# A two-layer sequence trunk on one core: the planner that orders its instructions gets measured durations instead of guessed ones

## The chip, the core and the metric

One core of a Trainium2 chip runs the whole program once. The metric is the device time of one execution in microseconds (us), the median over several. The engines are TensorE (PE), VectorE (DVE), ScalarE (ACT), GpSimd (POOL) and SyncE (SP); each works through its own instructions strictly in their order, and semaphores tie the engines together.

## What is computed

The input is 2048 tokens of 1024 channels in float32, the output the same. There are two layers with a residual each, and a last RMSNorm:

```
def _even_mixer(h, w_in, ...):                    # layer 0, h = rmsnorm(x)
    proj = jnp.einsum('bsd,de->bse', h, w_in)     # 1024 -> 2048
    u_pool, u_ssm, z = proj[..., :512], proj[..., 512:1024], proj[..., 1024:]
    y_pool = _multiscale_pool(u_pool, pool_w, pool_scale)   # windows 2, 4, 8, 16; 128 channels each
    y_ssm = _s5(u_ssm, ...)     # 32 groups of 16 channels, 64 complex states each, then a GLU
    y = jnp.concatenate([y_pool, y_ssm], axis=-1) * jax.nn.silu(z)
    return jnp.einsum('bse,ed->bsd', y, w_out)    # 1024 -> 1024

def _odd_mixer(h, w_in, ...):                     # layer 1
    val, gt, z = three times 1024 channels of h @ w_in
    g = val * jax.nn.sigmoid(gt)
    c = causal depthwise convolution of g, width 31, + conv_b
    c = layernorm(c) * ln_g + ln_b
    return (silu(c) * silu(z)) @ w_out
```

## The kernel before

**Tiling.** The sequence is worked in two halves, A and B, of 1024 tokens, each in two blocks of 512. A large product is cut into units of 128 output channels for one half. Each weight tile of 128x1024 is loaded (`raw`), cast to a rounded part on ACT and subtracted from the original on DVE, so that a high and a low part (`w`) exist; the activations are split alike. A unit then has 8 (contraction) x 3 (high x high, high x low, low x high) x 2 (blocks) = 48 matmuls of 128x128 by 128x512. Its sum lies in a PSUM slot `mm`, of which there are three, until DVE or ACT has evacuated it.

**PE's units** come in a written order, on the thread `main`: A.s0 to A.s3 (input of the SSM), A.pu0, A.pz0, A.pu1 ... A.pz3 (input of the pooling and its gate), A.z0 to A.z3 (gate of the SSM), the same for B; then A.glu, A.o (output projection of layer 0), A.g, A.v, A.y (layer 1), the same for B, and A.q, B.q (last projection; A.q.e0t0 is its first unit). The first three units of a projection are done block by block (A.s2.0, A.s2.1), as are A.z1 to A.z3. Some hundred smaller pieces of matmuls stand between and inside the units: the tables of the SSM (threads prepw and prepg), the SSM itself (ssm00 and 01 for half A, ssm10 to 12 for half B), the pooling (pool0, pool1), part of the convolution, and the sums of the LayerNorm (lnA0, lnA1, lnB0, lnB1: one for each block).

**What makes the order.** The kernel isn't written in the order in which it runs. Each thread is a generator that yields an operation (`Op`, with its engine, an assumed duration, what it reads and writes), a request for a slot (`Alloc`) or a condition (`Wait`). `Sched.run` plays the program: every engine has a clock (`clk`), `ready` gives the time at which an operation's operands are there, and `run` always takes the operation that can start first; among those of the same engine that can start within a small tolerance (`EPS`) it takes first the ones that aren't of `main`, then those of the higher rank. `emit` advances the clock and writes the instruction. So the durations decide nothing of what is computed, but in which order each engine gets its instructions, which slot each tile lies in, and where a piece stands among the units. On the chip the order is fixed, whatever the real durations are.

**Queues.** All DMAs, loads and stores, are issued by SP in the planned order (`dma`, L342). The slots that tie the engines beside `mm`: 2 `raw`, 8 `w` (four tiles of weights), 8 `st` (scratch), 2 `po` (evacuated sums), 25 `act`, 2 `aux` (PSUM of the small pieces).

**Places the text speaks of.** The SSM's tables are made on DVE from `ca`, `cg` and `pw` in scratch slots (`act16_...<-cg1_...`), sent through small matmuls and stored to DRAM (`Kd`, `Wd`, `Md`); the rates (`act17`, `rsc`) come first. `ud`, `upd`, `z0d` and `zp` are DRAM copies of evacuated units. A pooling step loads `upd`, sums on DVE, splits, loads `z0d`, and only then takes an `mm` slot, has six matmuls done in it, and evacuates it with a product by z0d (L308):

```
        yield dma(sz, z0d[h][gi])
        ps = yield Alloc("mm")
        yield mmb([... six matmuls into ps ...])
...
        yield stt(sz, ps, vc("pool_scale", gi), sz, ALU.mult, ALU.mult)
        free("mm", ps)
```

`rsd` holds the reciprocal norms of 1024 tokens; they are stored as single elements (`sml`, one float for each run) and loaded again, spread over all partitions.

In the profile L290 is DVE's two-operand operation, L308 the three-operand one, L318 the scan, L322 ACT's copy, L333 ACT's activation, L351 the matmul, L342 the DMA. In the changed kernel the same lines are L312, L330, L340, L344, L356, L390 and L375.

Of the kernel before, what the change touches and what calls it, by code (L numbers as in the profile page):

```python
# [73 lines left out]
class Sched:  # L74
# [132 lines left out]

    def run(self):
        while self.threads:
# [13 lines left out]
            est = lambda t: max(self.clk[t.op.eng], t.op.ready)  # L223
            first = min(cand, key=est)
            e0 = est(first)
            eng = first.op.eng
            near = [t for t in cand if t.op.eng == eng and est(t) <= e0 + self.EPS[eng]]
            th = min(near, key=lambda t: (t.bulk, t.prio, est(t)))
# [6 lines left out]
def trunk(ctx, tc, io):  # L235
# [49 lines left out]

    def tt(o, a, b, op, eng=None):
        if eng is G:
            return Op("G", 0.25 + width(o) * 2.1e-3, [a, b], [o], lambda: G.tensor_tensor(o, a, b, op))  # L288
        d = 0.13 + width(o) / 960.0 + (0.13 if isps(a, b) else 0.0)
        return Op("V", d, [a, b], [o], lambda: V.tensor_tensor(o, a, b, op))  # L290

    def ts(o, a, s1, s2=None, op0=ALU.mult, op1=None, eng=None):
# [8 lines left out]
        if eng is G:  # L301
            return Op("G", 0.25 + width(o) * 1e-3, rd, [o], emit)
        return Op("V", 0.15 + width(o) / (960.0 if isps(a) else 1920.0), rd, [o], emit)

    def stt(o, a, s, b, op0, op1):
        rd = [a, b] + ([s] if isinstance(s, bass.AP) else [])
        d = 0.13 + width(o) / 960.0 + (0.13 if isps(a, b) else 0.0)
        return Op("V", d, rd, [o], lambda: V.scalar_tensor_tensor(o, a, s, b, op0, op1))  # L308

    def vcopy(o, a):  # L310
        return Op("V", 0.13 + width(o) / 960.0, [a], [o], lambda: V.tensor_copy(o, a))

    def recip(o, a):
        return Op("V", 0.13 + width(o) / 120.0, [a], [o], lambda: V.reciprocal(o, a))

    def scan(o, r, x, ini):
# [1 line left out]
        return Op("V", 0.13 + width(o) / 480.0, rd, [o], lambda: V.tensor_tensor_scan(  # L318
            o, r.to_broadcast([128, width(o)]), x, ini, ALU.mult, ALU.add))

    def acopy(o, a):
        return Op("A", 0.05 + width(o) / 960.0, [a], [o], lambda: A.copy(o, a))  # L322

    def amul(o, a, m):
        return Op("A", 0.1 + width(o) / 960.0, [a], [o], lambda: A.mul(o, a, m))

    def act(o, a, fn, **kw):
# [9 lines left out]

    def dma(o, i):
        n = int(np.prod(o.shape)) * 4
        run = 4 * min(a.ap[-1][1] if a.ap[-1][0] == 1 else 1 for a in (o, i))  # L340
# [1 line left out]
        return Op("SP", slow * n / 360e3, [i], [o], lambda: SP.dma_start(out=o, in_=i))  # L342
# [19 lines left out]
    def trb(batch):  # L362
# [1443 lines left out]
```

## Time and profile before

| | us |
|---|---|
| median of three runs | 1537.63 (1532.89 to 1539.34) |
| the profiled execution, its own time | 1537.14 |
| its span, first instruction to last | 1535.3 |
| PE busy in the span | 1481.3 |
| DVE busy | 1128.9 |
| ACT busy | 524.2 |
| POOL busy | 103.6 |
| mean granted clock of PE | 0.991 |

A line of an engine's timeline gives the start and the length in us, the instruction with out<-in, and in brackets the idle time before it and whose result ended it. A line of waits reads: engine, tile and source line that waited, `<-` what it waited for: us in total, how often, the longest. A group reads: instructions of one kind, `|` busy us, mean ns of one `|` idle us before them. A bound engine that is busy for most of the span can only gain what it waits and what its clock loses.

### The profile page before, as it was taken

To read this page: it belongs to the slowest core of one execution; us is meant where nothing else is said; L and a number is where in the kernel's file an instruction comes from. 1 tells how busy PE (TensorE), PEld (TensorE's weight loads), DVE (VectorE), ACT (ScalarE), POOL (GpSimd) and SP (SyncE) were. 2 spreads that over 40 slices of the span, in tenths; PEclk is the share of its full clock that TensorE was granted. 3 is DMA by queue.
4 is the path that set the end of the run, shared out by engine and by line. 5 is a ranking of instruction groups with operands and counts; after the bars stand their busy time and mean duration, and the time that the engine had idled before them with its cause. 6 is when DMAs were issued, how large, how long until landed. Compare 5 with 4: busy or idle time off the path is not lost. (4 is left out here: it accounts for less than half of the span.)

```text
span 1535.3 us, 18361 instructions
## 1 busy us (share of the span) xinstructions
PE 1481.3 (96%) x6942; PEld 1213.6 (79%) x6942; DVE 1128.9 (74%) x1318; ACT 524.2 (34%) x829; POOL 103.6 (7%) x313
## 2 busy tenths in 40 slices
PE   5899979999999999999999999999999999999997
PEld 3678768788888888888888888888888888887785
DVE  7882648887877533399999999245997898967652
ACT  6113433122135225311111530352364465443431
POOL 1000010110000002000000000120000000003322
PEclk9999989999999999999999999999999999999999
DMA  8238966877775763223253442623476485956743
GB/s 302 96 97 235 331 193 216 266 239 263 239 252 191 207 229 124 83 83 110 82 111 122 179 164 97 220 83 111 98 177 204 133 284 172 363 206 222 257 158 116
DMA packets 165464, 280.77 MB, mean 183 GB/s; under 512 B 55712, under 2 KB 86144, under 8 KB 165376
## 3 DMA queue, kind: packets, MB, share of 16 engines
q1 hardware_dynamic: 165376, 279.61, 56.1%
q8 instruction: 54, 0.88, 0.2%
q14 instruction: 34, 0.28, 0.1%
HBM read 183.93 MB, written 91.43 MB: 179 GB/s over the span
## 5 line engine op out<-in xcount | busy, mean ns | idle before, releaser
L351 PE MATMUL mm<-act,w 128*128 128x512 f32 x4224 | 1002.3, 397 | 29.0 <-ACT w L322 11.1
L351 PEld LDWEIGHTS mm<-act,w 128*128 128x128 f32 x4224 | 793.1, 189 | 211.8 <-ACT w L322 11.1
L308 DVE SCALAR_TENSOR_TENSOR ca<-cg,cwt,ca 128x1024 f32<-128x1024 f32 (+1 forms) x360 | 397.8, 1106 | 14.5 <-ACT ca L333 4.2
L351 PE MATMUL mm<-w,act 128*128 128x512 f32 x1344 | 318.9, 397 | 1.4 <-DVE w L290 1.4
L351 PEld LDWEIGHTS mm<-w,act 128*128 128x128 f32 x1344 | 253.3, 189 | 60.8 <-DVE w L290 1.9
L322 ACT CAST w<-raw 128x1024 fp32r<-128x1024 f32 (+1 forms) x117 | 121.3, 1038 | 265.8 <-PE mm L351 207.2
L290 DVE TENSOR_TENSOR w<-raw,w 128x1024 fp32r<-128x1024 f32 (+1 forms) x117 | 141.6, 1212 | 51.4 <-ACT w L322 50.1
L333 ACT ACTIVATE junk<-st 128x1024 bf16<-128x1024 f32 (+1 forms) x64 | 54.0, 844 | 135.1 <-DVE st L290 122.3
L290 DVE TENSOR_TENSOR po<-mm,st 128x1024 f32<-128x1024 f32 x32 | 46.6, 1455 | 70.6 <-PE mm L351 65.6
L290 DVE TENSOR_TENSOR st<-st,mm 128x512 f32<-128x512 f32 x48 | 30.9, 684 | 76.0 <-PE mm L351 76.0
L322 ACT COPY st<-aux 128x512 f32<-128x512 f32 (+2 forms) x56 | 25.7, 471 | 129.5 <-PE aux L351 100.8
L322 ACT CAST act<-st 128x512 fp32r<-128x512 f32 (+1 forms) x64 | 51.8, 853 | 46.7 <-DVE st L308 16.6
L333 ACT ACTIVATE act<-act,mask 128x128 f32<-128x128 f32 x192 | 57.8, 390 | 18.8 <-DMA act<-band 18.8
L290 DVE TENSOR_TENSOR act<-st,act 128x512 fp32r<-128x512 f32 (+1 forms) x64 | 56.3, 920 | 3.5 <-ACT act L322 3.3
L308 DVE SCALAR_TENSOR_TENSOR st<-st,mm 128x1024 f32<-128x1024 f32 x24 | 34.4, 1432 | 25.8 <-PE mm L351 25.8
L333 ACT ACTIVATE st<-mm 128x1024 f32<-128x1024 f32 x24 | 24.6, 1026 | 83.2 <-PE mm L351 81.0
L308 DVE SCALAR_TENSOR_TENSOR act<-aux,vcol,act 128x512 fp32r<-128x512 f32 x32 | 22.5, 746 | 40.3 <-ACT act L333 40.3
L518 POOL TENSOR_TENSOR sml<-sml,mhalf 128x1 f32<-128x1 f32 (+2 forms) x38 | 28.0, 736 | 346.5 <-DVE sml L298 343.7
L290 DVE TENSOR_TENSOR st<-st 128x512 f32<-128x512 f32 (+4 forms) x44 | 41.2, 937 | 9.8 <-DMA st<-upd 8.4
L351 PEld LDWEIGHTS aux<-st,act 128*128 128x128 f32 x384 | 45.5, 192 | 2.9 <-ACT act L333 1.4
L351 PE MATMUL aux<-st,act 128*128 128x128 f32 (+1 forms) x384 | 45.5, 274 | 1.1 <-ACT act L333 1.0
L351 PE MATMUL mm<-act,act 128*128 128x512 f32 x192 | 44.9, 393 | 0.8 <-DVE st L290 0.8
(144 smaller groups left out, 937.7 us busy)
## 6 DMA issues: line engine op xcount, KB each, us to landing
raw<-in_odd_w_in SPq DMA_DIRECT2D x48, 512.0 KB, 3.7
raw<-in_even_w_in SPq DMA_DIRECT2D x31, 512.0 KB, 5.1
st<-x1d SPq DMA_DIRECT2D x48, 256.0 KB, 4.9
st<-in_xT SPq DMA_DIRECT2D x16, 512.0 KB, 6.0
st<-in_x SPq DMA_DIRECT2D x16, 512.0 KB, 9.0
raw<-in_even_w_out SPq DMA_DIRECT2D x16, 512.0 KB, 3.7
z1d<-po SPq DMA_DIRECT2D x16, 512.0 KB, 3.2
st<-z1d SPq DMA_DIRECT2D x16, 512.0 KB, 6.2
```

Of the source, the lines that this page charges most:

```text
L290: return Op("V", d, [a, b], [o], lambda: V.tensor_tensor(o, a, b, op))
L308: return Op("V", d, rd, [o], lambda: V.scalar_tensor_tensor(o, a, s, b, op0, op1))
L322: return Op("A", 0.05 + width(o) / 960.0, [a], [o], lambda: A.copy(o, a))
L333: return Op("A", (0.3 if len(wr) > 1 else 0.13) + width(o) / 960.0, rd, wr, lambda: A.activation(o, a, fn, **kw))
L351: nc.tensor.matmul(o, w, x, start=s, stop=e)
L518: yield Op("G", 0.3, [a], [o], lambda: G.tensor_tensor(o, a, mhalf[:, :n], ALU.pow))
```

## The change

The assumed durations are replaced. DVE, ACT and POOL operations get a fixed part and a rate each, with a factor where the innermost stride is 8 elements or more; two operations of DVE or ACT overlap by 0.08 or 0.1 us (`OVER`); an operation now also waits in the plan for a result of its own engine, except on PE; a matmul of 512 columns costs 0.231 us instead of 0.216 and its result is there 0.4 later; a DMA has three numbers (time on the shared rate, issue time of SP, landing), and one made of short runs costs time for each run: 8.7 ns for each single element. The choice in `run` is moved into a method `pick`, unchanged. Cut to its core (`ts`, `recip`, `scan`, `vcopy`, `gset`, transposes and `rsqrt_of` get new numbers in the same manner):

```
 class Sched:
+    OVER = {"PE": 0.0, "V": 0.084, "A": 0.1, "G": 0.0}
...
     def ready(self, op):
...
-                    if a < hi and lo < b and p0 < q1 and q0 < p1 and (wr or w) and (e != op.eng or e == "SP"):
-                        r = max(r, t + 0.1)
+                    if a < hi and lo < b and p0 < q1 and q0 < p1 and (wr or w) and not (e == op.eng == "PE"):
+                        r = max(r, t + 0.05)
...
     def emit(self, op):
         start = max(self.clk[op.eng], op.ready)
         if op.eng == "SP":
-            issue = start + 0.66
-            self.clk["SP"] = issue
-            self.dma = max(self.dma, issue) + op.dur
-            end = self.dma + 1.9
+            dur, issue, land = op.dur
+            self.clk["SP"] = start + issue
+            self.dma = max(self.dma, start + 0.5) + dur
+            end = self.dma + land
         else:
             end = start + op.dur
-            self.clk[op.eng] = end
+            self.clk[op.eng] = end - self.OVER[op.eng]
+            if op.eng == "PE":
+                end += 0.4
...
+    def far(*aps):
+        for a in aps:
+            pat = [p for p in a.ap[1:] if p[1] > 1]
+            if pat and abs(pat[-1][0]) >= 8:
+                return True
+        return False
+
+    def vdur(c, per, o, *aps):
+        return c + width(o) * per * (1.8 if far(o, *aps) else 1.0)
+
+    def adur(o, a, n):
+        return (0.18 if isps(a) else 0.2) + 0.09 * n + width(o) * (1.85e-3 if far(o, a) else 0.828e-3)
...
     def tt(o, a, b, op, eng=None):
...
-        d = 0.13 + width(o) / 960.0 + (0.13 if isps(a, b) else 0.0)
+        d = vdur(0.16, 1.035e-3, o, a, b)
...
     def stt(o, a, s, b, op0, op1):
...
-        d = 0.13 + width(o) / 960.0 + (0.13 if isps(a, b) else 0.0)
+        d = vdur(0.27, 0.935e-3, o, a, b) if isps(a, b) else vdur(0.2, 1.06e-3, o, a, b)
...
     def acopy(o, a):
-        return Op("A", 0.05 + width(o) / 960.0, [a], [o], lambda: A.copy(o, a))
+        return Op("A", adur(o, a, 0), [a], [o], lambda: A.copy(o, a))
...
     def dma(o, i):
         n = int(np.prod(o.shape)) * 4
         run = 4 * min(a.ap[-1][1] if a.ap[-1][0] == 1 else 1 for a in (o, i))
-        slow = 1.0 if run >= 512 else 1.5 if run >= 256 else 2.0
-        return Op("SP", slow * n / 360e3, [i], [o], lambda: SP.dma_start(out=o, in_=i))
+        rows = n // max(run, 4)
+        if run >= 1024:
+            d = n / 408e3
+        elif run >= 512:
+            d = n / 325e3
+        elif run >= 64:
+            d = rows * (2e-3 if run % 64 and o.space == bass.MemoryType.DRAM else 1.1e-3)
+        else:
+            d = rows * 8.7e-3
+        land = 1.0 if o.space == bass.MemoryType.DRAM else 1.9
+        return Op("SP", (d, 0.42 if rows <= 128 and n > 131072 else 0.6, land), [i], [o],
+                  lambda: SP.dma_start(out=o, in_=i))
 
     def mmb(batch):
-        d = sum(width(o) / 2400.0 if x.dtype == F32R else max(width(o), 128 if w.shape[1] > 64 else 0) / 600.0
-                for o, w, x, s, e in batch) + 0.0027 * len(batch)
+        d = 0.0
+        for o, w, x, s, e in batch:
+            if x.dtype == F32R:
+                d += width(o) / 2216.0
+            elif w.shape[1] > 64:
+                d += max(0.224, width(o) * 1e-3)
+            else:
+                d += 0.07 + width(o) * 0.5e-3
```

No instruction is added or removed; on every engine their order differs, except that `main`'s units keep theirs. Three places follow.

DVE, while PE works on A.s0 to A.s3, before: `po..<-mm..` are the evacuations of A.s0, A.s1 and A.s2, `w..<-raw..` splits of weights, the rest steps of the SSM's tables.

```order
L290 TENSOR_TENSOR po0_61_616<-mm0_46_377,st7_55_527 128x8x128
L290 TENSOR_TENSOR w1_63_618<-raw1_50_401,w0_62_617 128x1024
L290 TENSOR_TENSOR act19_60_585<-ca1_32_323,w2_35_326 128x256 x2
L290 TENSOR_TENSOR ca1_32_323<-act19_60_585 128x256
L290 TENSOR_TENSOR act19_60_585<-ca1_32_323,w2_35_326 128x256 x2
L290 TENSOR_TENSOR ca1_32_323<-act19_60_585 128x256
L290 TENSOR_TENSOR po1_65_654<-mm1_51_425,st7_55_527 128x8x128
L290 TENSOR_TENSOR w5_67_656<-raw0_52_494,w4_66_655 128x1024
L290 TENSOR_TENSOR act16_56_558<-cg1_34_325 128x512
L290 TENSOR_TENSOR cg1_34_325<-ca0_31_322,pw_271 128x512 x2
L290 TENSOR_TENSOR act16_56_558<-cg1_34_325 128x512
L290 TENSOR_TENSOR po0_70_692<-mm2_53_495,st7_55_527 128x8x128
```

The same place afterwards (the first half of `act16` stands six rows earlier):

```order
L312 TENSOR_TENSOR w1_62_604<-raw1_50_409,w0_61_603 128x1024
L312 TENSOR_TENSOR ca1_32_324<-act19_63_616 128x256
L312 TENSOR_TENSOR act16_56_569<-cg1_34_326 128x512
L312 TENSOR_TENSOR act19_63_616<-w2_35_327,ca0_31_323 128x256 x2
L312 TENSOR_TENSOR cg1_34_326<-ca0_31_323,pw_271 128x512
L312 TENSOR_TENSOR po0_60_602<-mm0_47_379,st0_55_532 128x8x128
L312 TENSOR_TENSOR po1_66_646<-mm1_51_423,st0_55_532 128x8x128
L312 TENSOR_TENSOR w5_68_648<-raw0_52_494,w4_67_647 128x1024
L312 TENSOR_TENSOR po0_71_682<-mm2_53_495,st0_55_532 128x8x128
L312 TENSOR_TENSOR w7_73_684<-raw1_64_628,w6_72_683 128x1024
```

The second half of the first pair of tables (`act16<-cg1`) now stands ahead of the first evacuation (`po0_60`); before, both halves stood behind the second (`po1_65`).

SP, the loads of weights for A.pu2 (`raw0`) and A.pz2 (`raw1`) before; `rsc` is the store of the rates, with which the stores of the tables begin:

```order
L342 DMA raw0_89_863<-in_even_w_in 128x1024
L342 DMA upd0_0_245<-po0_92_959 128x1040
L342 DMA raw1_95_979<-in_even_w_in 128x1024
L342 DMA st5_96_982<-upd0_0_245 128x1040
L342 DMA rsc_235<-act17_58_567 32x1x64 x6
L342 DMA z0d0_0_141<-po1_100_1034 128x1024
```

And afterwards, the last rows ahead of the same two loads; `rsc` stands 29 rows earlier:

```order
L375 DMA Md1_216<-st7_93_925 128x1024
L375 DMA st3_100_1031<-Kd2_233 128x1x128 x6
L375 DMA Kd3_234<-st1_94_945 128x256
L375 DMA Wd6_205<-act22_88_860 64x512 x2
L375 DMA Wd7_206<-act22_88_860 64x512 x2
L375 DMA z0d0_0_141<-po1_104_1085 128x1024
L375 DMA st5_114_1120<-Kd3_234 128x1x128 x3
L375 DMA Md2_217<-st4_101_1032 128x1024
L375 DMA st5_114_1120<-Kd3_234 128x1x128 x5
L375 DMA raw0_85_835<-in_even_w_in 128x1024
L375 DMA raw1_119_1172<-in_even_w_in 128x1024
```

The loads stood ahead of the rates and tables; they now stand behind the first 65 of these and other issues (an x and a number counts so many).

SP, the store of the norms and the load of z0d for the pooling step whose matmuls stand at A.z, before:

```order
L342 DMA st4_179_1689<-in_xT 128x1024
L342 DMA yd0_0_125<-st0_104_1074 128x4x128
L342 DMA rsd1_190<-sml2_149_1460 128x8x1
L342 DMA st6_98_1009<-z0d0_0_141 128x1024
L342 DMA st2_189_1761<-in_xT 128x1024
L342 DMA st0_185_1741<-rsd1_190 128x1024
```

Afterwards, first the load of z0d, and 33 rows further on the store of the norms:

```order
L375 DMA st6_148_1459<-in_pool_w 128x128
L375 DMA yd0_0_125<-st7_116_1164 128x4x128
L375 DMA act23_149_1474<-act22_129_1260 64x1024 x2
L375 DMA st3_123_1202<-z0d0_0_141 128x1024
L375 DMA yd0_0_125<-st1_117_1165 128x4x128
```

```order
L375 DMA st1_199_1816<-in_xT 128x1024
L375 DMA st4_201_1822<-in_xT 128x1024
L375 DMA rsd1_190<-sml2_172_1607 128x8x1
L375 DMA st6_207_1837<-in_pool_w 128x128
L375 DMA zp0_0_237<-po0_203_1830 128x1024
```

The load of z0d stood right behind the store `rsd`; now it stands well ahead of it, and behind the store stands a load of pooling weights.

More of the change, by code (lines that the diff above doesn't have):

```diff
@@ L206, in unblock, with pick @@
         return got[0] if b.n is None else got
+    def pick(self, cand):
+        est = lambda t: max(self.clk[t.op.eng], t.op.ready)
+        first = min(cand, key=est)
+        e0 = est(first)
+        eng = first.op.eng
+        near = [t for t in cand if t.op.eng == eng and est(t) <= e0 + self.EPS[eng]]
+        return min(near, key=lambda t: (t.bulk, t.prio, est(t)))
     def run(self):
@@ L222, in run @@
                     + str({k: len(v) for k, v in self.pools.items()}))
[L223 to L228, printed above, removed]
+            th = self.pick(cand)
             op, th.op = th.op, None
@@ L301, in ts @@
         if eng is G:
-            return Op("G", 0.25 + width(o) * 1e-3, rd, [o], emit)
-        return Op("V", 0.15 + width(o) / (960.0 if isps(a) else 1920.0), rd, [o], emit)
+            return Op("G", 0.19 + width(o) * 1e-3, rd, [o], emit)
+        return Op("V", 0.165 + width(o) * (1.03e-3 if isps(a) else 0.55e-3), rd, [o], emit)
     def stt(o, a, s, b, op0, op1):
         rd = [a, b] + ([s] if isinstance(s, bass.AP) else [])
-        d = 0.13 + width(o) / 960.0 + (0.13 if isps(a, b) else 0.0)
+        d = vdur(0.27, 0.935e-3, o, a, b) if isps(a, b) else vdur(0.2, 1.06e-3, o, a, b)
         return Op("V", d, rd, [o], lambda: V.scalar_tensor_tensor(o, a, s, b, op0, op1))
     def vcopy(o, a):
-        return Op("V", 0.13 + width(o) / 960.0, [a], [o], lambda: V.tensor_copy(o, a))
+        return Op("V", 0.15 + width(o) * 1e-3, [a], [o], lambda: V.tensor_copy(o, a))
     def recip(o, a):
-        return Op("V", 0.13 + width(o) / 120.0, [a], [o], lambda: V.reciprocal(o, a))
+        return Op("V", 0.14 + width(o) / 150.0, [a], [o], lambda: V.reciprocal(o, a))
     def scan(o, r, x, ini):
         rd = [r, x] + ([ini] if isinstance(ini, bass.AP) else [])
-        return Op("V", 0.13 + width(o) / 480.0, rd, [o], lambda: V.tensor_tensor_scan(
+        return Op("V", 0.2 + width(o) * 1.9e-3, rd, [o], lambda: V.tensor_tensor_scan(
             o, r.to_broadcast([128, width(o)]), x, ini, ALU.mult, ALU.add))
     def acopy(o, a):
-        return Op("A", 0.05 + width(o) / 960.0, [a], [o], lambda: A.copy(o, a))
+        return Op("A", adur(o, a, 0), [a], [o], lambda: A.copy(o, a))
     def amul(o, a, m):
-        return Op("A", 0.1 + width(o) / 960.0, [a], [o], lambda: A.mul(o, a, m))
+        return Op("A", adur(o, a, 0), [a], [o], lambda: A.mul(o, a, m))
     def act(o, a, fn, **kw):
@@ L332, in act @@
             wr.append(kw["accum_out"])
-        return Op("A", (0.3 if len(wr) > 1 else 0.13) + width(o) / 960.0, rd, wr, lambda: A.activation(o, a, fn, **kw))
+        n = sum(isinstance(s, bass.AP) for s in kw.values())
+        return Op("A", adur(o, a, n), rd, wr, lambda: A.activation(o, a, fn, **kw))
     def gset(o, v):
-        return Op("G", 0.25 + width(o) * 0.5e-3, [], [o], lambda: G.memset(o, v))
+        return Op("G", 0.1 + width(o) * 0.8e-3, [], [o], lambda: G.memset(o, v))
     def dma(o, i):
@@ L365, in emit @@
                 nc.tensor.transpose(o, a, idn)
-        op = Op("PE", 0.11 * len(batch), [b[1] for b in batch] + [batch[0][2]], [b[0] for b in batch], emit)
+        op = Op("PE", 0.105 * len(batch), [b[1] for b in batch] + [batch[0][2]], [b[0] for b in batch], emit)
         op.n = len(batch)
@@ L517, in rsqrt_of @@
         tv = t[:, :n]
-        yield Op("G", 0.3, [a], [o], lambda: G.tensor_tensor(o, a, mhalf[:, :n], ALU.pow))
+        yield tt(o, a, mhalf[:, :n], ALU.pow, G)
         yield tt(tv, o, o, ALU.mult, G)
```

3 lines of the change are left out of this document (2 added, 1 removed).

## The prediction

> **What bounds the kernel now.** I read the page first: which engine is busy, and whether its clock holds.
>
> ```profile
> PE 1481.3 (96%) x6942; PEld 1213.6 (79%) x6942; DVE 1128.9 (74%) x1318; ACT 524.2 (34%) x829; POOL 103.6 (7%) x313
> PEclk9999989999999999999999999999999999999999
> ```
>
> TensorE (PE) is busy for 96% of 1535.3 us, at nine tenths of its clock or more except in one slice. No matmul is removed, so a new order can only save what PE waits, and what its clock loses beside a wait. The view of PE's waits lists the first:
>
> ```profile
> PE mm L351 <- ACT w L322: 11.1, 1, 11.1
> PE mm L351 <- DVE st L308: 9.6, 1, 9.6
> PE mm L351 <- DVE w L290: 9.2, 3, 5.4
> PE aux L351 <- DVE act L290: 6.2, 6, 2.1
> PE aux L351 <- DVE st L290: 3.2, 2, 1.8
> PE aux L351 <- DMA act<-ud: 2.1, 3, 1.2
> ```
>
> These six rows hold 41.4 us: most of what there is. The timeline of PE says where (start, length, instruction, then the wait before it):
>
> ```profile
> 17.77 13.73 PE L351 MATMUL mm<-act,w 128*128 128x512 f32 x48 [5.41 <-DVE w L290]
> 33.82 5.34 PE L351 MATMUL mm<-act,w 128*128 128x512 f32 x22 [2.32 <-DVE w L290]
> ...
> 60.16 0.57 PE L351 MATMUL aux<-act,cg 128*32 128x112 f32 x2 [2.09 <-DVE act L290]
> 62.88 0.40 PE L351 MATMUL aux<-act,cg 128*32 128x112 f32 x1 [2.14 <-DVE act L290]
> ...
> 82.43 0.37 PE L351 MATMUL aux<-act,cg 128*32 128x112 f32 x1 [0.56 <-DVE act L290]
> ...
> 168.79 1.16 PE L351 MATMUL aux<-act,st 128*128 128x128 f32 x8 [1.23 <-DMA act<-ud]
> ...
> 215.44 37.35 PE L351 MATMUL mm<-act,w 128*128 128x512 f32 x150 [9.61 <-DVE st L308]
> ```
>
> The first two waits for weights (11.1 and 5.41) belong to the first loads and splits, whose places stay; both remain. The clock comes from a table of windows (length, PE, PEld, DVE, ACT, POOL, granted clock, DMA share, GB/s):
>
> ```profile
> 64.50:70.10 5.60, 5.60 (x19) 4.27 (x18) 5.53 (x7) 0.27 (x1) 0.00 (x0) 0.75 0.56 187
> 215.44:219.00 3.56, 3.56 (x8) 2.84 (x9) 1.41 (x2) 1.19 (x2) 0.00 (x0) 0.50 1.00 335
> 219.00:223.60 4.60, 4.60 (x18) 3.71 (x17) 1.54 (x2) 1.05 (x2) 0.00 (x0) 0.79 0.68 262
> 1400.00:1460.00 60.00, 55.37 (x231) 44.04 (x230) 42.41 (x46) 22.21 (x35) 21.48 (x51) 0.94 0.69 227
> ```
>
> After the 9.61 us wait the clock is 0.50, then 0.79: 3.56 x 0.50 + 4.60 x 0.21 = 2.7 us are lost beside the wait itself. After the pair of 2.1 us waits it is 0.75: 5.60 x 0.25 = 1.4 us. Between 1400 and 1460 us full speed would need 55.37 x 0.94 = 52.0 of 60 us: 8.0 are lost.
>
> **The change, part by part.** All instructions stay; on every engine they come in another order. PE's own units keep theirs; what moves is the small work between them and the queues of DVE, ACT, POOL and SP. A place in the new order is read from the built programs, a duration always from the trace of before.
>
> *1, weights of A.s2.* The wait of 2.32 us at 33.82 is for the DVE half of a split. That split keeps its place in DVE's row, but the table chain that stood ahead of it, each step waiting for the one before, is now interleaved with a second chain, so those waits are filled; by the durations it ends at about 31, before PE arrives. **-2.3.**
>
> *2, the tables of the SSM between A.s3 and A.pu0.* PE's first table pieces come 6 matmuls into the second half of A.s3, while DVE still works on the evacuations of A.s0 to A.s2 (2.1 us each). Five waits from 60.16 to 82.43 are the result: the row of 6.2 less its sixth (0.4, below), 5.8 us, and 1.4 of clock. Afterwards DVE makes the first of these tables before those evacuations, and PE takes the pieces after 42 matmuls of A.s3, and later. 7.2 go; I keep 1.5 (from 0 to 4) for evacuations that are late instead, since more of the three PSUM slots are then full at once. **-5.7.**
>
> *3, SP's queue and the weights of A.pu2.* All loads and stores are issued by SP, in order:
>
> ```profile
> 106.67 3.87 SPq L342 DMA_DIRECT2D rsc<-act  x6
> ...
> 137.66 1.07 SPq L342 DMA_DIRECT2D raw<-in_even_w_in  x2
> ```
>
> Between these two rows stand 47 issues in 31.0 us, 0.66 each. Here they stand behind the fetches for A.pu2 and A.pz2; afterwards 65 such issues stand ahead of them. They can begin when the rates are made:
>
> ```profile
> 50.58 2.27 DVE L290 TENSOR_TENSOR po<-mm,st 128x1024 f32<-128x1024 f32 x1 [4.99 <-DMA st<-rsd]
> ...
> 129.97 1.23 DVE L290 TENSOR_TENSOR po<-mm,st 128x1024 f32<-128x1024 f32 x1 [8.79 <-PE mm L351]
> 141.16 1.22 DVE L290 TENSOR_TENSOR po<-mm,st 128x1024 f32<-128x1024 f32 x1 [9.96 <-PE mm L351]
> ```
>
> From the first evacuation at 50.58 DVE has 18.2 us of work up to the rates: 68.8. Then 65 x 0.66 = 42.9, so the fetch is issued at 111.7. It lands 5.1 later (row below), and the two steps of the split take 1.0 and 1.2: 119.1. PE begins A.pu2 where A.pz1 ends, at 129.97 before; less terms 1 and 2 that is 122. So the weights are there, with 3 us to spare, but DVE, whose row has the split at a fixed place, stands still for about 7 us in front of it. Behind it stand the SSM's products for the pieces in A.pz2. The two rows above show DVE waiting 8.79 and 9.96 us for PE there, which would cover the 7; but the new order fills such gaps with SSM work. Between 0 and 8 us I take 3. The 1.23 at 168.79 goes, some 1 us of such waits comes in its place. **+2.8.**
>
> *4, the stall at A.z3.* At 215.44 PE waits 9.61 us for a PSUM slot. The first pooling step holds it, whose DVE step waits for a load of z0d:
>
> ```profile
> raw<-in_even_w_in SPq DMA_DIRECT2D x2, 512.0 KB, 5.1
> ...
> st<-z0d SPq DMA_DIRECT2D x1, 512.0 KB, 13.8
> rsd<-sml SPq DMA_DIRECT2D x1, 4.0 KB, 9.8
> ```
>
> (The first row is of the DMA issues from 100 to 140 us, the others of those from 180 to 220.) The 4 KB store rsd goes out in single elements and takes 9.8 us; z0d, issued right behind it, takes 13.8 where a load of that size takes 5.1. Afterwards z0d is loaded 33 rows of SP before rsd, and what stands behind rsd is a load for the next pooling step. The 9.6 and the 2.7 of clock go. That next step could hold a slot in the same way, but the slot is wanted 54 matmuls, 12.6 us, later, more than the 9.8. **-12.3.**
>
> By the Trainium skill ("TensorE: Matmul & The Clock Gate", Part 1: The HAM clock gate) the clock halves after an idle window of about 3.4 us, and is whole again after about 3.4 us of work. The 0.50 over 3.56 us behind the long wait agrees. The 0.75 behind two waits of 2.1 us does not follow from it; by the rule alone term 2 would be 1.4 smaller, and the span 1.4 longer.
>
> *5, the SSM of half B.* The waits of PE from 224 to 480 us:
>
> ```profile
> PE aux L351 <- DMA act<-ud: 0.9, 2, 0.7
> PE aux L365 <- DVE act L290: 0.7, 1, 0.7
> PE aux L351 <- ACT st L322: 0.7, 1, 0.7
> PE mm L351 <- DVE act L290: 0.5, 1, 0.5
> PE aux L351 <- DVE act L290: 0.4, 1, 0.4
> ```
>
> 3.2 us, all in places that move. What comes instead is DVE's load, priced with groups from 365 to 480 us:
>
> ```profile
> L351 PE MATMUL mm<-act,w 128*128 128x512 f32 x397 | 95.4, 396 | 0.5 <-DVE act L290 0.5
> L351 PE MATMUL aux<-act,act 128*128 128x128 f32 x64 | 12.4, 275 | 0.0
> L351 PE MATMUL aux<-act 128*128 128x128 f32 x64 | 12.4, 275 | 0.0
> L351 PE MATMUL aux<-act,st 128*128 128x128 f32 x64 | 8.4, 274 | 0.0
> ...
> L290 DVE TENSOR_TENSOR st<-aux,act 64x512 f32<-64x512 f32 (+1 forms) x24 | 16.5, 688 | 2.7 <-PE mm L351 2.2
> L318 DVE TENSOR_TENSOR_SCAN st<-r8t,zini,st 128x127 f32<-128x127 f32 x32 | 12.8, 463 | 0.2
> ...
> L290 DVE TENSOR_TENSOR po<-mm,st 128x1024 f32<-128x1024 f32 x8 | 9.8, 1222 | 12.5 <-PE mm L351 12.5
> ```
>
> One unit of 48 matmuls takes 141.16 - 129.97 = 11.19 us, 0.233 each. The 397 take 92.5 of the 115 us, and 22.5 are left for 17 pieces (8 of eight small matmuls, 8 of sixteen, one of pooling): 1.32 each. Afterwards, from the evacuation of B.pz0 to the piece behind B.pz2, DVE has 32 scans (32 x 0.463 = 14.8), 60 products (x 0.688 = 41.3), 8 evacuations and splits (x 1.222 = 9.8) and 5 smaller steps (about 1.8): 67.7 us. PE has 186 matmuls (43.3) and 15 pieces (19.8): 63.1. DVE ends 4.6 later; I take 4 (0 to 10, as it may be hidden by pieces in reserve, or met again in the next round). 4 - 3.2: **+0.8.**
>
> *6, LayerNorm of half B.* The 8.0 us of 1400 to 1460 are waits for LayerNorm's sums (3.2) and for weights (1.4), and their clock. The last block's first sum on PE is moved from late in A.q to the first unit of A.q, 300 matmuls or 70 us earlier; the first block's by 60 matmuls, 14 us. DVE's work ahead of the latter is the same within 2 us, so DVE has to make up 14 us in the convolution's stretch, out of waits like these of 1050 to 1345 us:
>
> ```profile
> DVE w L290 <- ACT w L322: 17.6, 7, 9.0
> ```
>
> The other rows of that view hold 15 more. If DVE makes them up, nothing waits; if not at all, 14 us are paid. I take 2: **-8.0 + 2 = -6.0.**
>
> The tail behind the last matmul keeps its steps: 0.
>
> **Sum.** -2.3 - 5.7 + 2.8 - 12.3 + 0.8 - 6.0 = -22.7. The span goes from 1535.3 to 1512.6. The profiled execution took 1537.14, 1.84 around its span and 0.5 under the median of 1537.63, so I forecast **1514 us**.
>
> **Rivals.**
> *All of the new waits are hidden* (terms 3, 5 and 6 cost nothing, 3 + 1 + 4 + 2 = 10 less, and 1.5 less in term 2): 1503. For it speaks that DVE is only 74% busy; against it, that its free time lies in the waits for PE, where its order pins it.
> *DVE becomes the bound of SSM and LayerNorm.* The new order lays both closer to DVE's limit. At the far ends of terms 5 (10) and 6 (10 of 14) it costs 6 + 8 = 14 more: 1528, from 1521 to 1533. For it: 67.7 against 63.1 us, and nothing between that could absorb an error of 5% in DVE's durations.
> *Bunched waits.* If the new waits come in pairs of 2 us, each pair costs 1.4 of clock besides, as at 64.50. Four such places: 1520. By the Trainium skill's idle window ("TensorE: Matmul & The Clock Gate", Part 1), such pairs would cost no clock at all.
> *SP's queue ends it, slower than before.* If the 65 issues take longer than 0.66 us each, because they wait for tables that DVE makes late, PE stands at A.pu2. Each 0.1 us is 6.5 us. There are 3 us to spare, so it starts at 0.71; it eats the whole gain of 22.7 from about 1.06, and gives 1541 at 1.11. Against it: in the 31 us quoted SP did 0.66 with the same tables in work.
> That nothing changes is excluded: the orders differ on every engine.
>
> **How the numbers follow.** The sum 0.55 (1506 to 1521), all hidden 0.14 (1499 to 1506), DVE the bound 0.20, bunched 0.05, SP's queue 0.06. From 1500 to 1530 all but the last and a third of DVE's case lies, 0.86. A measurement of this kernel can tell about 0.5%, 7.7 us: faster means below 1529.9. Faster: 0.55 + 0.14 + 0.05 + 0.13 = 0.87; slower 0.06; the rest of DVE's case, 0.07, is the same.
>
> **What the profile afterwards would show.** Term 4: no wait over 2 us in A.z0 to A.z3, and a clock of 1.0 there. Term 2: at most 1.5 us of waits in the table pieces between 50 and 90 us. Term 3: the fetches for A.pu2 issued at 105 to 118 us, a DVE wait before that split, and a PE wait at A.pz2. Term 5: PE waiting for DVE in B.pu3. Term 6: between A.q.e0t0 and the end of A.q the clock at 1.0 and waits below 3 us. Unchanged: 11.1 and 5.4 at the start, and the tail. Wrong it would be through a long PE wait on a load that the new queue of SP has put behind others, a cause that these terms price only at A.pu2.

## The result: 0.8% slower instead of 1.5% faster

The changed kernel takes 1547.78 us in the median (1546.54 to 1549.63, five runs), the kernel before 1535.50 beside it (1532.89 to 1539.34): a ratio of 1.0079, 95% interval 1.0058 to 1.0100. The forecast was 1514 us, with 1500 to 1530 as its range. The span of the profiled execution went from 1535.3 to 1544.8.

The page of the changed kernel, and its waits of PE (engine, tile and line `<-` what ended the wait: us in total, times, longest):

```profile
PE 1483.0 (96%) x6942; PEld 1211.3 (78%) x6942; DVE 1123.3 (73%) x1318; ACT 522.1 (34%) x829; POOL 92.8 (6%) x313
```

```profile
PE aux L390 <- DMA act<-ud: 17.5, 5, 8.1
PE mm L390 <- ACT w L344: 11.3, 1, 11.3
PE mm L390 <- DVE w L312: 8.1, 4, 5.3
PE aux L390 <- DVE st L312: 7.4, 4, 2.1
PE aux L390 <- DMA st<-Gd: 2.8, 2, 1.5
PE aux L390 <- DVE act L312: 2.3, 4, 0.7
```

PE's work grew by 1.7 us only; its waits went from 45.1 to 52.6 (all rows of the two views added). The waits that the forecast meant to end in half A did end: the 9.6 behind z0d has no row, the 2.32 for the weights of A.s2 is gone, and of the 6.2 for `act` from DVE 0.32 is left in the tables (the 2.3 of the row above stand in pieces of the SSM). But 17.5 us of waits for loads of `ud` stand where 2.1 were, 2.8 for `Gd`, which had none, and 7.4 for LayerNorm's sums where 3.2 were. PE's timeline has the places:

```profile
65.24 0.30 PE L390 MATMUL aux<-ca,cg 128*32 128x16 f32 x4 [0.32 <-DVE act L333]
...
128.62 2.04 PE L390 MATMUL aux<-act,st 128*128 128x128 f32 x8 [8.08 <-DMA act<-ud]
...
247.10 1.36 PE L390 MATMUL aux<-act,st 128*128 128x128 f32 x8 [3.47 <-DMA act<-ud]
...
290.61 1.13 PE L390 MATMUL aux<-act,st 128*128 128x128 f32 x8 [2.69 <-DMA act<-ud]
...
386.76 1.13 PE L390 MATMUL aux<-act,st 128*128 128x128 f32 x8 [1.50 <-DMA st<-Gd]
...
1342.31 1.10 PE L390 MATMUL aux<-st,onesN 128*128 128x512 f32 x2 [2.03 <-DVE st L312]
...
1354.08 1.10 PE L390 MATMUL aux<-st,onesN 128*128 128x512 f32 x2 [2.15 <-DVE st L312]
```

The clock follows the waits (a table of windows as in the prediction):

```profile
128.62:132.00 3.38, 3.38 (x12) 3.08 (x13) 3.31 (x5) 0.55 (x1) 0.00 (x0) 0.52 1.06 382
132.00:136.00 4.00, 4.00 (x22) 3.36 (x21) 3.57 (x5) 0.00 (x0) 0.00 (x0) 1.00 0.80 321
208.00:224.00 16.00, 15.49 (x76) 12.77 (x75) 3.83 (x7) 4.33 (x8) 0.00 (x0) 1.00 0.83 228
1342.31:1345.80 3.49, 3.49 (x9) 2.47 (x10) 1.13 (x2) 0.00 (x0) 0.00 (x0) 0.68 1.04 400
1345.80:1349.30 3.50, 3.50 (x14) 2.78 (x14) 3.31 (x3) 0.00 (x0) 0.00 (x0) 0.83 1.04 408
```

At A.z3 (third row) PE works through at full clock, as forecast. The 8.08 us wait is followed by 3.4 us at 0.52, then 1.00. The 2.03 us wait of LayerNorm costs 3.49 x 0.32 + 3.50 x 0.17 = 1.7 us of clock beside itself.

To see where time went, the time that PE lost is counted by stage: the growth of (start of a unit in the trace) less (PE's own work ahead of it, with 0.2306 us for a large matmul and the lengths of the small pieces as in the trace before). It holds waits and clock together, and doesn't change when a piece only moves. (A stage can come out slightly below 0, since the lengths of before hold some slow clock.) The last unit's sum is 73.0 us before and 82.1 after, 9.1 more, which is what the spans differ by within 0.4.

| stage | before | after | measured | forecast |
|---|---|---|---|---|
| start to A.s3 | 22.8 | 20.0 | -2.8 | -2.3 (term 1) |
| A.s3 to A.pu2 | 8.7 | -0.6 | -9.3 | -5.7 (term 2) |
| A.pu2 to A.z0 | 1.9 | 14.4 | +12.5 | +2.8 (term 3) |
| A.z0 to the second round of A.z1 | 12.9 | 1.2 | -11.7 | -12.3 (term 4) |
| from there to A.glu0 | 6.5 | 17.4 | +10.9 | +0.8 (term 5) |
| A.glu0 to B.y4 | 8.3 | 11.5 | +3.2 | 0 |
| B.y4 to B.q.e1t1 | 10.6 | 16.7 | +6.1 | -6.0 (term 6) |
| to the last unit | 1.3 | 1.6 | +0.3 | 0 |

The gains came, 23.8 us instead of 20.3 in terms 1, 2 and 4. They were given back mostly by pieces of the SSM and of LayerNorm that reach PE before their operands.

### The profile page after: what moved, and what is told of

It reads as the page before. It is cut to its first block, busy times and chain, and to the rows that moved or that the text cites. A ratio compares the mean times of both kernels' runs of the same rounds, so it can differ in the third digit from the quotient of the medians.

```text
span 1544.8 us, 18374 instructions
## 1 busy us (share of the span) xinstructions
PE 1483.0 (96%) x6942; PEld 1211.3 (78%) x6942; DVE 1123.3 (73%) x1318; ACT 522.1 (34%) x829; POOL 92.8 (6%) x313
## 5 line engine op out<-in xcount | busy, mean ns | idle before, releaser
L330 DVE SCALAR_TENSOR_TENSOR ca<-cg,cwt,ca 128x1024 f32<-128x1024 f32 (+1 forms) x360 | 397.8, 1106 | 22.8 <-ACT ca L356 12.3
L312 DVE TENSOR_TENSOR act<-st,act 128x512 fp32r<-128x512 f32 (+1 forms) x64 | 57.0, 927 | 14.5 <-ACT act L344 14.4
L312 DVE TENSOR_TENSOR st<-st 128x512 f32<-128x512 f32 (+4 forms) x44 | 41.0, 936 | 15.7 <-DMA st<-upd 14.4
L390 PEld LDWEIGHTS aux<-st,act 128*128 128x128 f32 x384 | 45.1, 192 | 2.9 <-ACT act L356 1.7
L330 DVE SCALAR_TENSOR_TENSOR st<-st,mm 128x1024 f32<-128x1024 f32 x24 | 34.2, 1425 | 17.9 <-PE mm L390 17.5
L312 DVE TENSOR_TENSOR st<-aux,act 64x512 f32<-64x512 f32 (+1 forms) x48 | 33.0, 687 | 18.9 <-issue 9.2
```

The lines of the kernel that those rows point to most:

```text
L390: nc.tensor.matmul(o, w, x, start=s, stop=e)
```

## What the plan itself says

The planner's own clock, set beside the trace, shows how the two orders differ. It is the time at which the plan lets a unit start:

| unit | before: plan | trace | late by | after: plan | trace | late by |
|---|---|---|---|---|---|---|
| A.pu2 | 114.9 | 129.8 | 14.9 | 115.6 | 117.6 | 1.9 |
| A.pz2 | 125.2 | 140.9 | 15.7 | 129.4 | 141.2 | 11.9 |
| B.s0.0 | 205.2 | 240.3 | 35.1 | 219.6 | 236.5 | 17.0 |
| A.glu0 | 412.6 | 464.2 | 51.6 | 439.6 | 469.7 | 30.1 |
| B.glu0 | 799.0 | 877.9 | 78.9 | 845.6 | 877.5 | 31.9 |
| last | 1386.9 | 1514.3 | 127.4 | 1474.3 | 1523.3 | 49.0 |

Before, PE ran some 7% faster in the plan than on the chip, so PE fell behind the plan, between A.glu0 and B.glu0 by 27.3 us in 36 units, about 0.76 us each. Everything that the plan had made ready for a piece had that much more time. Afterwards the plan is right about PE: between A.glu0 and B.glu0 it is off by 1.8 us in 407. So it sets a piece at the very matmul at which its operands come due. Where it is late now, it is late by a jump, and the jump is a wait of PE with the slow clock behind it (from A.pu2 to A.pz2 10.0 us, of which 8.08 are the wait below).

The first jump is the 8.08 us in A.pu2. SP's timeline of the changed kernel:

```profile
65.21 3.88 SPq L375 DMA_DIRECT2D rsc<-act  x6
...
108.37 1.06 SPq L375 DMA_DIRECT2D raw<-in_even_w_in  x2
109.53 4.12 SPq L375 DMA_DIRECT2D act<-act  x4
...
118.92 0.45 SPq L375 DMA_DIRECT2D act<-Wd  x1
119.66 0.37 SPq L375 DMA_DIRECT2D act<-ud  x1
```

and from the DMA issues between 115 and 131 us (the first row is the share of the 16 engines, the others KB each and us to landing):

```profile
q1 hardware_dynamic: 2671, 5.77, 104.0%
...
raw<-in_even_w_in SPq DMA_DIRECT2D x3, 512.0 KB, 8.3
...
act<-ud SPq DMA_DIRECT2D x2, 256.0 KB, 7.8
```

The 65 issues take 43.2 us, 0.664 each; the plan has 0.60 for most of them. It lets the first load of `ud` be issued at 109.9; the chip does so at 119.66, with the DMA engines at a share of 104%, and the two loads of `ud` in that window take 7.8 us in the median. The piece is due at 120.5.

## Experiments

Two theories from the start. **M (no slack):** PE's true rate in the plan takes away the slack that covered every other error. **Q (the queue):** the new numbers for SP's issues and for landings are at fault by themselves. Each kernel was timed in three rounds against the kernel before on the same chip (1533.65 to 1535.83 us there). Ratios are to that kernel.

**1. The changed kernel with PE planned as before.**

```
-                d += width(o) / 2216.0          # and the small matmuls
+        d = sum(width(o) / 2400.0 if x.dtype == F32R else ... / 600.0 ...) + 0.0027 * len(batch)
-            if op.eng == "PE":
-                end += 0.4
```

> The changed kernel, but the plan's matmuls last as before (0.216 us instead of 0.231, no 0.4 us until the result), so that PE in the plan is 7% faster than on the chip. Theory M (no slack): a plan with PE at its true rate sets each small piece at the very matmul at which its operands come due, and any lateness becomes a wait of PE; with PE too fast in the plan every piece stands later than it need. M expects 1514 to 1526 us, the waits of PE for loads of ud below 4 us (17.5 in the changed kernel), those for LayerNorm's sums below 4 (7.4). Theory Q (the queue): the fault is in the new numbers of SP's issues and landings alone; it expects the wait in A.pu2 to stay at 6 us or more and 1538 to 1550.

1516.79 us, ratio 0.9887 (0.9873 to 0.9902). As M had it, but for one part: waits for ud fell from 17.5 to 8.5, not below 4; LayerNorm's sums to 3.7.

**2. The kernel before with PE planned at its true rate, nothing else.**

```
+                d += width(o) / 2216.0
+            if op.eng == "PE":
+                end += 0.4
```

> The kernel before with nothing changed but the plan's durations of matmuls and transposes (0.231 us, result 0.4 later). M: the slack of the old plan goes, and waits for the SSM's operands and LayerNorm's sums appear: 1545 or more. Q: the queue is planned as before, so nothing is lost: 1528 to 1540.

1577.40 us, ratio 1.0289 (1.0272 to 1.0305). PE's durations alone are brought nearer the truth, and 42 us are lost: the waits of PE add up to about 75 us, 45 in the kernel before. That they had covered errors of the plan elsewhere is how M reads it.

**3. The changed kernel with a margin for PE.**

```
-                        r = max(r, t + 0.05)
+                        r = max(r, t + (8.0 if op.eng == "PE" and e == "SP" else 1.0 if op.eng == "PE" else 0.05))
```

> The changed kernel with all of its new durations, and a margin for PE: in the plan a PE instruction starts no sooner than 8 us after the landing of a load that it reads and 1 us after the end of another engine's work (0.05 for both in the changed kernel). M: 1515 to 1526, waits for loads below 4 us; the waits for LayerNorm's sums (not loads) only a little better than 7.4. Q: the same for the loads, 1520 to 1532.

1543.91 us, ratio 1.0067 (1.0052 to 1.0082): both theories missed. The waits for ud went (1.6 us), and others came that hadn't been there:

```profile
138.15 3.33 PE L390 MATMUL mm<-st,pwt 128*128 128x512 f32 x6 [5.28 <-ACT st L344]
...
246.97 12.98 PE L390 MATMUL mm<-act,w 128*128 128x512 f32 x45 [5.50 <-ACT act L356]
```

Ending the waits for loads was not enough (against Q), and a margin on what PE reads didn't do what a PE planned too fast does for all chains (against M as it was put here).

**4. The changed kernel, loads planned to land later.**

```
-        land = 1.0 if o.space == bass.MemoryType.DRAM else 1.9
+        land = 1.0 if o.space == bass.MemoryType.DRAM else 5.0
```

> The changed kernel, with loads planned to land 5 us behind their transfer instead of 1.9, for all engines alike. Q: the loads were planned too early by 3 to 6 us each, so nearly all of the 17.5 us of waits for ud go: 1518 to 1530. M: PE has slack towards loads only, LayerNorm's waits stay: 1526 to 1538.

1521.43 us, ratio 0.9913 (0.9897 to 0.9930), where Q expected it. Waits for ud: 6.8. Stage A.pu2 to A.z0 loses 8.4 instead of 14.4. LayerNorm's first sums don't wait (M had them stay), but one wait for weights of 6.99 us stands there. So 26 us of the changed kernel's time go without a change to PE's numbers: slack on the loads does it too.

**5. The first pieces of the SSM held back to A.pz3.**

```
+        if h == 0 and u < 2:
+            yield Wait(("u", "A.pz3"))
         ss = yield Alloc("aux")
```

> The changed kernel; the first two pieces of the SSM (one each of ssm00 and ssm01) may not start before A.pz3, so they stand 528 matmuls into PE's work instead of 396 and 414 (546 and 594 in the kernel before). LayerNorm's pieces stand exactly where they stand in the changed kernel. If the loads behind SP's 65 issues are what costs 8 us of wait and some 2 of clock in A.pu2, those go and the later waits for ud shrink with them: 1528 to 1538. If those loads are late anyway, the wait moves to A.pz3: 1543 or more. LayerNorm's waits stay at 7 us.

1550.50 us, ratio 1.0095 (1.0073 to 1.0117). The wait moved:

```profile
132.22 1.09 PE L404 MATMUL aux<-ident,act 128*128 128x128 f32 x4 [5.85 <-DVE act L312]
...
203.41 2.08 PE L390 MATMUL aux<-act,st 128*128 128x128 f32 x8 [5.73 <-DMA act<-ud]
```

Holding one piece back lets the planner fill the place with the next thing that it believes ready.

**6. The last LayerNorm sum held back to A.q.e1t2.**

```
+        if h == 1 and b == 1:
+            yield Wait(("u", "A.q.e1t2"))
         mups = yield Alloc("aux")
```

> The changed kernel; the first sum of the last LayerNorm block waits for the unit A.q.e1t2, so it stands 5280 matmuls into PE's work (4998 in the changed kernel, 5298 before). All pieces of the SSM stand exactly where they stand in the changed kernel. M: the 8.2 us that the LayerNorm part loses against before come from putting that sum 70 us earlier than DVE can serve: 1538 to 1543, one wait of about 2 us left there. If DVE's load is the bound whatever the order (theory L), the waits only move: 1545 to 1550.

1550.42 us, ratio 1.0098 (1.0079 to 1.0117). The sum of the other block, which stayed where it was, now waits 6.20 us where it had waited 2.15:

```profile
1353.09 2.05 PE L390 MATMUL aux<-st,onesN 128*128 128x512 f32 x2 [6.20 <-DVE st L312]
```

DVE, in turn, waits for loads of the convolution's result (`cd`) in the 8 us ahead of it. First this run, then the changed kernel:

```profile
1345.46 1.22 DVE L312 TENSOR_TENSOR st<-act,act 128x1024 f32<-128x1024 f32 x1 [2.53 <-DMA act<-cd]
1348.01 1.22 DVE L312 TENSOR_TENSOR st<-st,act 128x1024 f32<-128x1024 f32 x1 [1.32 <-DMA act<-cd]
1351.00 1.23 DVE L312 TENSOR_TENSOR st<-st,act 128x1024 f32<-128x1024 f32 x1 [1.76 <-DMA act<-cd]
```

```profile
1345.66 1.23 DVE L312 TENSOR_TENSOR st<-act,act 128x1024 f32<-128x1024 f32 x1 [2.36 <-DMA act<-cd]
...
1348.21 1.23 DVE L312 TENSOR_TENSOR st<-st,act 128x1024 f32<-128x1024 f32 x1 [0.19 <-DMA act<-cd]
...
1350.98 1.23 DVE L312 TENSOR_TENSOR st<-st,act 128x1024 f32<-128x1024 f32 x1 [0.42 <-DMA act<-cd]
```

The three steps start at the same times within 0.2 us, though DVE does less between them in this run. So for this block the loads of `cd` set the time of the sum, and PE, which had no wait at the sum held back, only stands there sooner. M's guess for this run fails; "DVE's load is the bound" comes out 0.4 us above its range, and DVE stands idle there.

**7 and 8. Half of PE's error back; SP's issues as measured.**

```
-                d += width(o) / 2216.0
+                d += width(o) / 2290.0
```

> The changed kernel with the plan's large matmuls at 0.2236 us, halfway between 0.216 and 0.231, all else new (results 0.4 us later too). M: half of the slack: between the 1516.8 of the first run and the 1547.8 of the changed kernel, 1522 to 1540. Q: no difference from the changed kernel, 1543 to 1552.

1538.47 us, ratio 1.0028 (1.0011 to 1.0045), within M's range; the waits for ud are 12.3.

```
-... 0.42 if rows <= 128 and n > 131072 else 0.6 ...
+... 0.42 if rows <= 128 and n > 131072 else 0.66 ...
```

> The changed kernel with 0.66 us for each small issue of SP instead of 0.60, as the trace shows it. Over 65 issues the plan is then 3.9 us later. Q: the wait in A.pu2 and its followers go with it, 1528 to 1538. M: only some 4 us of the 8 go, and LayerNorm's waits stay: 1540 to 1546.

1540.21 us, ratio 1.0027 (1.0014 to 1.0040). The first wait for ud went from 8.08 to 4.88, 3.2 less, where 65 x 0.06 = 3.9 was expected; the others add up to 9.3 (9.4 in the changed kernel), LayerNorm's sums to 5.7 (7.4). It is the lower end of M's range.

**9 to 11. More slack still.** Run 1's kernel with loads landing 4 us later; run 1's with the 0.4 us kept; and run 1's with a matmul of 0.2027 us:

```
-        land = 1.0 if o.space == bass.MemoryType.DRAM else 1.9     # run 9, to run 1's kernel
+        land = 1.0 if o.space == bass.MemoryType.DRAM else 4.0
+            if op.eng == "PE":                                      # run 10
+                end += 0.4
-        d = sum(width(o) / 2400.0 if x.dtype == F32R else ...       # run 11
+        d = sum(width(o) / 2560.0 if x.dtype == F32R else ...
```

> The changed kernel with the plan's old matmul durations (as in the first run) and loads planned to land 4 us behind their transfer instead of 1.9. M: both kinds of slack add, as they cover different waits: the waits for ud (8.5 in the first run) fall below 4, LayerNorm's stay below 4: 1506 to 1515. If the slack of the first run was enough and more only moves work about: 1516 or more.

> The first run's kernel, but a result of PE is again taken to be there 0.4 us later, so that only the 0.216 us for a matmul is old. M: the rate carries the slack, the 0.4 us is nothing: 1513 to 1521. If half of the first run's gain was the 0.4: 1528 or more.

> The first run's kernel with 0.2027 us for a matmul in the plan, so PE is 14% too fast in it. M: waits for ud and for LayerNorm's sums go below 4 together; but here the load of z0d stands only four rows of SP behind the store of the norms, so a wait of 3 to 8 us may come back in A.z. 1508 to 1522. If too much slack costs as much as too little: 1525 or more.

1526.17 us (0.9935, 0.9911 to 0.9959), 1516.82 (0.9866, 0.9831 to 0.9900) and 1545.18 (1.0064, 1.0039 to 1.0090). The 0.4 us is nothing; the matmuls' durations are what matters. But the other two miss M: more slack is not better. For the loads it is, in order: with 0.2311, 0.2236, 0.216 and 0.2027 us for a matmul the waits for ud are 17.5, 12.3, 8.5 and 3.4 us (but see run 16 for the first step). With 0.2027, however, other pieces come so late that what needs their results stands:

```profile
205.81 7.26 PE L382 MATMUL mm<-act,w 128*128 128x512 f32 x21 [7.53 <-DVE st L328]
...
1371.94 1.22 PE L382 MATMUL mm<-w,act 128*128 128x512 f32 x2 [10.33 <-ACT act L342]
```

The first is the stall behind z0d again (its load is four rows of SP behind the norms' store there), the second PE waiting in A.q for activations that come from the late LayerNorm.

**12 to 15. All combinations.** The change has three groups of numbers: PE; DMA; and the other engines (with the smaller changes in `ready` and `OVER`). Run 12 is the changed kernel with DMA's undone, run 13 undoes PE's too (as in run 1), run 14 is the kernel before with DMA's new, run 15 adds PE's (as in run 2):

```
-            dur, issue, land = op.dur                  # undone in 12 and 13, made in 14 and 15
-            self.clk["SP"] = start + issue
-            self.dma = max(self.dma, start + 0.5) + dur
-            end = self.dma + land
+            issue = start + 0.66
+            self.clk["SP"] = issue
+            self.dma = max(self.dma, issue) + op.dur
+            end = self.dma + 1.9
...                                                     # and the durations in dma()
```

> The changed kernel with DMAs planned as before (0.66 us for each issue, the old transfer rates, landing 1.9 us later), everything else new, PE at its true rate. Q: the new numbers of the queue are what costs, so the wait in A.pu2 and its followers go: 1518 to 1532. M: PE still has no slack: 1540 or more.

> The new durations of DVE, ACT and POOL alone; PE and the DMAs planned as before. With PE new and DMAs old the time was 1532.3, with PE old and DMAs new 1516.8. M (PE at its true rate takes the slack away): 15 to 30 us below 1532.3, so 1502 to 1518. If the new DMA numbers are needed for the gain at A.z3: the 9.6 us wait is back, 1520 to 1532.

> The new DMA numbers alone; PE and the other engines planned as before. PE keeps its slack, so no loss is due: 1518 to 1540 by M. The load of z0d is now issued ahead of the store of the norms, one row, so the wait of 9.6 us at A.z3 should go: lower half of that. Q (the DMA numbers cost by themselves): 1542 or more.

> New numbers for PE and DMAs, the other engines planned as before. PE's alone gave 1577.4. M: PE without slack and the other engines planned too fast or too slow: 1560 to 1590. Q adds its cost to that: 1585 or more. If the DMA numbers mend what PE's spoil: below 1560.

| other engines | DMA | PE as before | PE at its true rate | PE's numbers cost |
|---|---|---|---|---|
| before | before | 1535 (the kernel before) | 1577.40 | +42 |
| before | new | 1535.59 (1.0006, 0.9990 to 1.0022) | 1581.56 (1.0308, 1.0262 to 1.0354) | +46 |
| new | before | 1513.35 (0.9861, 0.9834 to 0.9887) | 1532.34 (0.9978, 0.9962 to 0.9994) | +19 |
| new | new | 1516.79 | 1547.78 (the changed kernel) | +31 |

The rows without a ratio are runs 1 and 2 and the kernels compared. PE's true rate costs 19 to 46 us in each of the four pairs. The new durations of DVE, ACT and POOL gain 19 to 45 in each of theirs (1535 to 1513, 1577 to 1532, 1536 to 1517, 1582 to 1548). The DMA numbers give nothing where PE has its old rate (0 and +3) and cost 4 and 15 where it has not. The waits for ud grow by both: by PE's numbers from 2.1 to 9.8, 9.4 to 15.3, 0 to 4.8 and 8.5 to 17.5 us (in the order of the table), by the DMA numbers from 2.1 to 9.4, 9.8 to 15.3, 0 to 8.5 and 4.8 to 17.5. So Q has a part in the changed kernel's loss, but only together with PE's numbers. Run 12 missed M's range and ended 0.3 us above Q's: with PE at its true rate the old DMA numbers leave 2.9 us of loss from A.pu2 to A.z0 where the new ones leave 14.4. Run 13 lies in M's range. Run 15 does too, and misses Q's. Run 14 lies in M's range, but not in its lower half: the wait at A.z3 came back as 6.74 us, though z0d's load was issued one row, 3.31 us, ahead of the norms' store. It still took 12.1 us, so a place just ahead of that store is not always enough. The longest waits of PE in run 13, the best:

```profile
PE mm L372 <- ACT w L342: 14.7, 2, 11.2
PE mm L372 <- DVE w L310: 3.6, 3, 2.0
PE aux L372 <- DVE act L310: 2.2, 1, 2.2
PE aux L372 <- DVE st L310: 1.9, 1, 1.9
```

No row for ud is left, and none for z0d. It is 34 us faster than the changed kernel and 22 faster than the kernel before.

**16. The scatter of an order.**

```
-                d += width(o) / 2216.0
+                d += width(o) / 2222.0
```

> The changed kernel with 0.2304 us for a matmul of 512 columns in the plan instead of 0.2311, a difference that means nothing, but gives another order (pieces move by up to 260 matmuls). It shows the scatter of an order. M and Q: 1538 to 1556, waits for ud and LayerNorm's sums of the same size though at other places. If the changed kernel's loss is bad luck of one order: anything from 1515 to 1560.

1556.06 us, ratio 1.0141 (1.0106 to 1.0177): 8 us slower than the changed kernel by an edit that means nothing. The upper end of M and Q was just missed. A wait of 7.72 us for DVE stands in A.z that the changed kernel doesn't have. The waits for ud are 12.0 us instead of 17.5: 5.8 in their row, and the first, 6.19, which the view puts down to an ACT copy that ended as the load landed, at 128.29. So the step from 17.5 to 12.3 in run 7 is no more than the scatter. And two orders that differ by less than about 10 us say little on their theories (runs 3, 5, 6, 7 and 8 against the changed kernel, 9 against 1). The four pairs above, all of one sign and 19 us or more, say more; but one pair of orders is all that the scatter is known from.

## Why the prediction was wrong

**The reading of the bound, and what goes, were right.** PE is busy for 96% in both; nothing but waits and clock moved. Term 1 gave -2.8 for -2.3, term 4 -11.7 for -12.3, term 2 -9.3 for -5.7: the new PSUM worry of 1.5 us was 0.32, and the lost clock around the pieces was more than the 1.4 of one window (from 56.3 to 64.5 us the clock before was 0.76 too). The prediction's own sign of being wrong, a long PE wait on a load that the new queue has put behind others, is what came.

**Term 3 failed in the step from the queue to PE.** The queue was right within 4 us: issues from 65.2 (forecast 68.8), 0.664 us each (0.66), the fetch at 108.4 (111.7), DVE standing still for 5.57 + 1.68 = 7.3 us (7) in front of two splits:

```profile
106.70 1.22 DVE L312 TENSOR_TENSOR po<-mm,st 128x1024 f32<-128x1024 f32 x1 [3.93 <-PE mm L390]
113.50 1.23 DVE L312 TENSOR_TENSOR w<-raw,w 128x1024 fp32r<-128x1024 f32 x1 [5.57 <-ACT w L344]
116.41 1.23 DVE L312 TENSOR_TENSOR w<-raw,w 128x1024 fp32r<-128x1024 f32 x1 [1.68 <-ACT w L344]
```

But I followed the queue only to the weights. Some ten issues behind them, at 119.66, stands the first load of the first SSM piece, and that piece had moved into A.pu2 itself (396 matmuls into PE's work, 546 before); the 3 us were put on DVE's work for the pieces in A.pz2, where PE doesn't wait at all. In place of these 3 us came 8.08 and 1.6 of clock (3.38 x 0.48), and 1.57 and 1.65 for two later loads of `ud`, where 1 was allowed. The rival "SP's queue ends it" named this queue, this unit and an end of 1541 or more, and got a chance of 0.06, because it was tied to the weights and to a slower issue, neither of which happened; that the time came out on its side is no proof of its mechanism.

**Term 5 failed in what it priced.** One stretch of DVE was worked out, 4 us late; PE waited 1.77 us for DVE in half B (0.60, 0.47, 0.70). The cost was loads: 3.47, 2.69, 1.27 and 1.50 us, and some 1.7 of clock behind the first (0.60 over 3.90 us). The first two are for pieces of half A's SSM that stand among B's units, which no term worked out. Every one of these loads had moved ahead with its piece, and none was checked. +0.8 became +10.9.

**Term 6 failed in taking DVE's idle time as free.** DVE's waits from 1050 to 1345 us in the changed kernel:

```profile
DVE ca L330 <- ACT ca L356: 11.6, 2, 10.6
DVE w L312 <- ACT w L344: 10.5, 6, 5.2
DVE st L312 <- DMA st<-z1d: 5.0, 5, 1.7
DVE st L312 <- DMA act<-cd: 2.1, 4, 1.0
```

All rows together are 33.5 us, against 33.1 before: of the 14 us that DVE was to make up out of its waits, none came out of them. The idle time is the time that its fixed order waits for others, and a new order has its own. -6.0 became +6.1, and 3.2 more ahead of B.y4, where the sum of half A's first block waits 1.89. For the block of run 6 the loads of `cd` are what its sum waits for, as shown there; for the sum at 1342.31 DVE works without a gap from 1337.70 on, and what made it late isn't settled. A run that loads `cd` earlier wasn't tried. In the built order the two blocks of half B have changed places, the last one's first sum 30 matmuls ahead of the first one's, which so comes only 30 earlier than before, not 60. The term also let the wait for weights in the last projection (1.4 before) go with LayerNorm's, without a reason. Three such waits stand there now, 2.9 us, one of them with a clock of 0.51 over the 3.50 us from 1446.00 behind it:

```profile
1445.89 7.37 PE L390 MATMUL mm<-w,act 128*128 128x512 f32 x24 [2.08 <-DVE w L312]
```

**The rest of the working.** No rival asked the question that decides here: what had covered the errors of the old plan? The numbers for it were in the diff, 0.216 us for a matmul against the 0.233 that I worked out myself from the evacuations. Instead, the changed order was judged only at the places where the old one had waited. (The 0.5 us by which the profiled execution lay under the median had to be added in the last step of the sum, which then gives 1514.9 and not 1514; that changes nothing.) That PE's numbers cost the time is shown by runs 1 and 2 and the two other pairs: taking them back gains 31 us, bringing them alone costs 42. They are not the only way to give the loads time: run 4 gains 26 us and leaves them as they are. That what they take away is slack is shown best for the loads of ud, whose waits grow with PE's numbers in all four pairs (by 4.8 to 9.0 us, where run 16's edit moved them by 5.5); for other chains it is argued from the same pairs.

The Trainium skill ("TensorE: Matmul & The Clock Gate", Part 1: The HAM clock gate) has the clock halved after an idle window of about 3.4 us and whole after as long a busy one. The 8.08 us wait agrees: 0.52 for 3.38 us, then 1.00. The wait of 2.03 us does not follow from a single idle window of that length, and was still followed by 0.68 and 0.83; here the measurement decides, and a wait of 2 us may cost nearly twice itself. It need not: behind the waits of 2.15 and 2.69 us the clock was 1.00.

## What to carry to other kernels

In this kernel a planner that puts work on an in-order engine needed slack, and a wrong duration gave it: before correcting one, ask which errors it covered, and correct the engines that feed first and the bound engine last. Slack given by name has to be tried: later landings gained 26 us (run 4), a margin on what PE reads 4 (run 3), no more than the scatter. When a step of a queue is moved, follow the queue past the first load that is needed, to every consumer behind it, and look where that consumer now stands. Idle time of an engine with a fixed order is not a reserve: before it is spent on paper, show that the order lets it be used.

## What the runs showed of the hardware

SP's issue is not a constant. The 65 issues took 0.664 us each, while single issues between waits take 0.32 to 0.38 (`y1d`, `z1d` and others), and the four issues at 109.53, at a DMA share of 0.91, took 4.12 us; why isn't shown. Between 115 and 131 us, at a share of 104%, loads of 256 KB landed 7.8 us after their issue in the median, and of 512 KB 8.3, where 5.1 was the median of the same weights before. Near the 4 KB store in single elements, loads of 512 KB can be slow on both sides: 13.8 us right behind it (before), 12.1 when issued 3.31 us ahead of it (run 14), but 4.6 for one issued 2.13 us ahead of it in the changed kernel; what decides isn't shown. And this PE-bound kernel has a scatter of some 8 us between the medians of two orders that differ by 0.3% in one planned duration; the runs of one order spread over 3 us in one case (1546.54 to 1549.63) and 11 in the other (1551.31 to 1562.58).
